# The recurrence's output copy behind the state's transposition and scaling, and the memory attention's Newton steps on VectorE

## The chip, the cores and the metric

The kernel runs on one core of one Trainium2 chip. The metric is the device time of one execution in microseconds (us), the median over several executions. The engines that matter are TensorE (PE, its weight loads shown apart as PEld), VectorE (DVE), ScalarE (ACT), GpSimd (POOL) and SyncE (SP, which issues the DMAs).

## The reference, cut to what matters

Two blocks follow each other, with 512 tokens of width 1024. The first mixes attention over the tokens and a context with a convolution. The second, with which this change has most to do, runs a delta-rule recurrence over 12 heads of width 64, beside it an attention of the tokens over 256 memory tokens, then an output projection and a feed-forward network.

```
def step(S, inp):                        # the recurrence, one token
    r_t, w_t, k_t, v_t, a_t, b_t = inp
    sa = einsum('bhvk,bhk->bhv', S, a_t)
    S = (S * w_t[:, :, None, :] + sa[..., None] * b_t[:, :, None, :]
         + v_t[..., None] * k_t[:, :, None, :])
    return S, einsum('bhvk,bhk->bhv', S, r_t)

def memory_cross_attention(q_mem, k_mem, v_mem, q_g, k_g):
    q = rms_norm_2(q_mem.reshape(B, T, MEM_HEADS, MEM_HEAD_DIM), q_g)
    k = k_mem * k_g                      # k_mem is rms-normed too
    s = einsum('bthd,bmhd->bhtm', q, k) * MEM_HEAD_DIM ** -0.5
    return einsum('bhtm,bmhd->bthd', softmax(s), v_mem)
```

## The kernel before, in words

Float32 products are made as three fp32r products of a high and a low part (`mm3`, `proj`), so each weight block (`wr`, by DMA) is split by ACT into `wh` and by DVE into `wl`. All instructions are given to a scheduling layer, which follows the order of the source by priority but moves an instruction past others where it reckons that an engine would wait; it also adds the semaphores. Within one PSUM bank it puts the accesses of any two engines one behind the other, in the order of the source. An engine works through its own list strictly in order, so an instruction that waits holds up all that stand behind it. Any edit to one engine's work can shift places in the lists of all.

The program has three stages in the trace: the first block (0 to 331 us), the second block's recurrence with the memory attention (331 to 767 us), and the feed-forward network (to 1120 us).

**The recurrence** runs over six pairs of heads, eight chunks of 64 tokens each. `gen_abc` makes each chunk's matrices (tiles `f`, `UX`, `E`, `W`, `QG`), and `gen_chain` carries the state from chunk to chunk. Its step works in one PSUM tile `yp` (tag `y`, a single buffer): four products of `E` and `UV` and one of the state `st` with `QG` give 64 columns of output and 64 of new state. Then DVE masks the state columns into `sb`, ACT copies the output columns into `y` (a tile `x` in the trace), PE transposes `sb` back into columns 128 to 255 of the same `yp`, and DVE scales that into the next `st`. The next step's products need the single `yp` free. There are 48 steps, 42 with a transposition. A table of due times (`CHAIN`, `TAIL` and others) sets the order in which the source emits these pieces among projections and the tail.

**The memory attention** (`memory`, in the tail) projects the memory tokens (`pj<-p`), takes `rm`, the memory rows' factor, then `rq` for the queries (16 columns) and `rk` for the keys (8 columns), both through `newton`, an inverse square root by three Newton steps, in 15 instructions on 128 x n tiles (tag `nr`). The first is always on DVE, the other 14 are on the engine that it is given: two to set up and four for each step. Both calls give it GpSimd. DVE then scales the keys by `rk` (`kn`, tag `p`, eight instructions and two copies). Three other calls of `newton` matter: the first block's attention (44 columns, on DVE), the first pair's `prep` (8 columns, on DVE), and the other pairs' `prep` and `finish` on GpSimd.

Of the kernel before, what the change touches and what calls it, by code (L numbers as in the profile page):

```python
# [16 lines left out]
AF = mybir.ActivationFunctionType  # L17
ALU = mybir.AluOpType
# [112 lines left out]
def flat(x):  # L131
    n = len(x.shape)
    if n == 2:
        return x
    if n == 3:
        return x.rearrange("p a b -> p (a b)")
    return x.rearrange("p a b c -> p (a b c)")
# [61 lines left out]
class SumSq:  # L199
# [12 lines left out]
    def rstd(self, ptag, inv, eps, r, eng=None):  # L212
        k = self.k
        n = self.w // P
        ss = k.t(ptag)
        for t in range(n):
            k.T.matmul(ss[:, t:t + 1], self.prev[:, t * P:(t + 1) * P], inv, start=True, stop=True)
        if eng is None:
            rsqrt(k, r, ss[:, :n], eps)
        else:  # L220
            newton(k, eng, r, ss[:, :n], eps)
        return r
# [7 lines left out]
def newton(k, G, r, x, eps=None, floor=None):  # L230
    n = x.shape[-1]
    xe, h, y, t = (k.t("nr", [n]) for _ in range(4))
    k.V.tensor_scalar(out=xe, in0=x, scalar1=floor if eps is None else eps, scalar2=None, op0=ALU.max if eps is None else ALU.add)
    G.tensor_scalar(out=h, in0=xe, scalar1=-0.5, scalar2=None, op0=ALU.mult)
    G.tensor_scalar(out=y.bitcast(I32), in0=xe.bitcast(I32), scalar1=-0.5, scalar2=float(0x5f3759df), op0=ALU.mult, op1=ALU.add)
    for i in range(3):
        G.tensor_tensor(out=t, in0=y, in1=y, op=ALU.mult)
        G.tensor_tensor(out=t, in0=t, in1=h, op=ALU.mult)
        G.tensor_scalar(out=t, in0=t, scalar1=1.5, scalar2=None, op0=ALU.add)
        G.tensor_tensor(out=r if i == 2 else y, in0=y, in1=t, op=ALU.mult)  # L240


class Norm:
# [96 lines left out]
def block1(k, I, st, h1d):  # L340
# [291 lines left out]
    for i in range(4):  # L632
# [4 lines left out]
        zgates(1)  # L637
    nrq = k.cal([32])
    newton(k, V, r44, ss44, 1e-6)
    V.tensor_scalar(out=rq, in0=rq, scalar1=0.125, scalar2=None, op0=ALU.mult)  # L640
    V.tensor_scalar(out=nrq, in0=rq, scalar1=-1.0, scalar2=None, op0=ALU.mult)
# [224 lines left out]
def prep(k, p, pd, wa, lw):  # L866
# [6 lines left out]
    for t in range(4):  # L873
        T.matmul(kss[:, 2 * t:2 * t + 2], sq[:, t * P:(t + 1) * P], k.sel2, start=True, stop=True)
    rn = k.t("s8", [8])
    newton(k, k.G if p else k.V, rn, kss[:, 0:8], floor=1e-24)
    yield
    ps = k.t("pj")
# [209 lines left out]
def gen_chain(k, p, pd, gi):  # L1088
    A, V, T = k.A, k.V, k.T
    mm = T.matmul  # L1090
    if gi == 0:
        pd["y"] = k.x()
    y = pd["y"]
    for cc in range(4 * gi, 4 * gi + 4):
        n, c = (cc // 2) % 2, cc % 2
        E, UV4, QG = pd[("g", gi)]
        yp = k.t("y")
        for h in range(2):
            u = 2 * h + n
            mm(yp[h * 64:h * 64 + 64, 0:P], UV4[:, u, c, :], flat(E[:, 2 * u + c]), start=True, stop=cc == 0)  # L1100
        if cc > 0:
            mm(yp[:, 0:P], pd["st"], QG[:, n, c, :], start=False, stop=True)
        if cc < 7:
            sb = k.t("sb", [2, 64])
            V.tensor_tensor(out=sb, in0=yp[:, 64:128].rearrange("p (o d) -> p o d", o=1).to_broadcast([P, 2, 64]),
                            in1=k.maskS.rearrange("p (c d) -> p c d", c=2), op=ALU.mult)
        A.activation(y[:, cc * 64:(cc + 1) * 64], yp[:, 0:64], AF.Copy)
        if cc < 7:
            T.transpose(yp[:, 128:256], flat(sb), k.ident)
            pd["st"] = k.t("st", [P])  # L1110
            V.tensor_scalar(out=pd["st"], in0=yp[:, 128:256], scalar1=pd["pc"][:, cc:cc + 1], scalar2=None, op0=ALU.mult)
        yield


# [27 lines left out]
def memory(k, I, qd, ssq, W):  # L1142
    A, V, T, Y = k.A, k.V, k.T, k.Y
# [22 lines left out]
    rm = ss.rstd("i", k.inv1k, 1e-6, k.cal([2]))  # L1166
    ssk = k.cal([8])
    rk, rq, nrq = k.cal([8]), k.cal([16]), k.cal([16])
    newton(k, k.G, rq, ssq, 1e-6)
    V.tensor_scalar(out=rq, in0=rq, scalar1=0.125, scalar2=None, op0=ALU.mult)  # L1170
    V.tensor_scalar(out=nrq, in0=rq, scalar1=-1.0, scalar2=None, op0=ALU.mult)
    kvs = []
    for t in range(2):
# [3 lines left out]
        sq = k.t("z", [4, 64])  # L1177
        A.activation(flat(sq), kv[:, :256], AF.Square, scale=0.125)
        V.tensor_reduce(out=ssk[:, 4 * t:4 * t + 4], in_=sq, op=ALU.add, axis=AX.X)
    newton(k, k.G, rk, ssk, 1e-6)  # L1180
    yield
    kns = []
    for t in range(2):
        kn = k.t("p", [4, 2, 64])
        for h in range(4):
            V.scalar_tensor_tensor(out=kn[:, h, 0, :], in0=kvs[t][:, h * 64:(h + 1) * 64], scalar=rk[:, 4 * t + h:4 * t + h + 1],
                                   in1=k.gg, op0=ALU.mult, op1=ALU.mult)
# [88 lines left out]
def block2(k, I, nm, h1d, out):  # L1276
# [47 lines left out]
    def tail():  # L1324
# [29 lines left out]
        Y.dma_start(out=gw, in_=I["g2"])  # L1354
        yield
        mem = memory(k, I, qd, ssq, W)
        for _ in range(10):
            next(mem)
# [26 lines left out]
    for p in range(6):  # L1385
        b = 2 * L * p
        at(prep(k, p, pds[p], wa, lw), *[b + r for r in PREP])
        at(project(p), *[b + LEAD[p] + PJ[0] + PJ[1] * i for i in range(3 * PIECES)])
        for gi in range(2):
            r0 = b + gi * L  # L1390
            at(gen_abc(k, p, pds[p], gi), *[r0 + i for i in range(16)])
            at(gen_chain(k, p, pds[p], gi), *[r0 + r for r in CHAIN])
        at(finish(k, p, pds[p]), *[b + L + r for r in FINISH])
# [215 lines left out]
```

## Time and profile before

| | |
|---|---|
| Time, median of 3 runs | 1121.05 us (1117.35 to 1123.47) |
| The profiled execution | 1122.11 us, span 1120.3 us |
| Mean granted TensorE clock | 0.986 |
| PE / DVE / ACT / POOL busy | 1077.6 / 727.6 / 538.0 / 61.8 us |

The span goes from the first to the last instruction of the profiled execution; 1.8 us of its time lie outside it. PE is busy nearly all the time, so what is to be read is when it is not, and when its clock is not full.

### The profile page before, as it was taken

What the parts mean: (1) busy time and instruction counts of PE and PEld (TensorE: products, weight loads), DVE (VectorE), ACT (ScalarE), POOL (GpSimd) and SP (SyncE); (2) the same over time, 40 slices, a digit from 0 to 9 for tenths busy, and PEclk for the clock granted to TensorE, in tenths of its full rate; (3) what the DMA queues carried; (4) which work ended last, traced back from release to release, by engine and by line L of the source; (5) the groups of instructions that cost most, each with busy time, mean ns of one, the idle gap of its engine ahead of it and who ended that gap; (6) DMA issues with size and microseconds to landing.
All of it is one profiled execution on the core that took longest, in us unless ns stands there. A gap on an engine that the chain in (4) does not pass through costs nothing.

```text
span 1120.3 us, 15945 instructions
## 1 busy us (share of the span) xinstructions
PE 1077.6 (96%) x6272; PEld 831.9 (74%) x6272; DVE 727.6 (65%) x1267; ACT 538.0 (48%) x987; POOL 61.8 (6%) x209
## 2 busy tenths in 40 slices
PE   8999989999999999999999879999999999999998
PEld 4668966666787677777777657768888888888887
DVE  3369999995776889797867877666444344344332
ACT  5444546765655556555455655555333133134110
POOL 0000000000010201122101121010000000000000
PEclk9999999999999999999999998999999999999999
DMA  9753221001362110110011212122323333333332
GB/s 330 286 178 105 64 81 45 1 23 35 94 199 90 57 39 20 39 37 28 32 39 52 67 48 76 40 74 85 104 94 94 94 96 101 103 95 94 94 122 85
DMA packets 32203, 96.46 MB, mean 86 GB/s; under 512 B 3456, under 2 KB 6272, under 8 KB 32128
## 3 DMA queue, kind: packets, MB, share of 16 engines
q1 hardware_dynamic: 32128, 95.45, 26.5%
q8 instruction: 49, 0.80, 0.3%
q14 instruction: 26, 0.21, 0.1%
HBM read 91.24 MB, written 4.19 MB: 85 GB/s over the span
## 4 chain that ended last, share of the span: by engine, by line
PE 82%; DVE 6%; ACT 4%; POOL 3%; DMA 3%; issue 2%; SPq 0%; ACTq 0%; DVEq 0%; POOLq 0%
PE pf L57 31%; PE pj L57 22%; PE s L57 9%; PE i L57 7%; PE pt L57 5%; PE pv L57 4%; PE y L57 3%; POOL nr L57 3%; DMA modw<-w_mod 1%; ACT p L57 1%; DVE wl L57 1%; DVE hg L57 1%; ACT wh L57 1%; DVE p L57 1%; DMA wr<-w_in 1%
## 5 line engine op out<-in xcount | busy, mean ns | idle before, releaser
L57 ACT ACTIVATE wh<-wr 128x1024 fp32r<-128x1024 f32 (+1 forms) x132 | 137.7, 1043 | 183.7 <-PE pf L57 73.9
L57 DVE TENSOR_TENSOR wl<-wr,wh 128x1024 fp32r<-128x1024 f32 (+1 forms) x132 | 158.7, 1203 | 21.9 <-PE pt L57 10.2
L57 PE MATMUL pf<-A,wh 128*128 128x512 f32 x512 | 157.8, 389 | 0.0
L57 PE MATMUL pj<-hg,wh 128*128 128x512 f32 x448 | 152.5, 412 | 1.4 <-DVE x L57 0.9
L57 ACT ACTIVATE f<-i 128x512 f16<-128x512 f32 (+1 forms) x132 | 71.9, 598 | 90.1 <-PE i L57 89.9
L57 PEld LDWEIGHTS pf<-A,wh 128*128 128x128 f32 x512 | 96.0, 188 | 19.7
L57 PE MATMUL pf<-A,wl 128*128 128x512 f32 x256 | 99.6, 389 | 0.0
L57 DVE TENSOR_TENSOR x<-x,pf 128x512 f32<-128x512 f32 (+1 forms) x33 | 22.2, 671 | 113.9 <-PE pf L57 113.9
L57 PEld LDWEIGHTS pj<-hg,wh 128*128 128x128 f32 x448 | 80.2, 190 | 18.5 <-issue 2.2
L57 PE MATMUL pj<-hg,wl 128*128 128x512 f32 x224 | 90.2, 403 | 0.0
L57 DVE SCALAR_TENSOR_TENSOR hg<-hg,c 128x499 f32<-128x499 f32 (+14 forms) x120 | 84.9, 738 | 0.7 <-ACT hg L57 0.4
L57 PE MATMUL pf<-ff,wh 128*128 128x512 f32 (+1 forms) x272 | 79.6, 377 | 0.0
L57 PE MATMUL pf<-hg,wh 128*128 128x512 f32 x256 | 78.8, 389 | 0.0
L57 DVE SCALAR_TENSOR_TENSOR fr<-pf,r 128x512 f32<-128x512 f32 x32 | 22.1, 691 | 85.4 <-PE pf L57 82.1
L57 ACT ACTIVATE fr<-fr 128x512 f32<-128x512 f32 x32 | 20.2, 632 | 99.9 <-DVE fr L57 99.9
L57 PEld LDWEIGHTS <-f 128*128 128x128 f16 x720 | 46.8, 101 | 24.1 <-issue 13.7
L57 PE MATMUL i<-f 128*128 128x128 f16 x672 | 56.2, 226 | 5.3 <-DVE f L57 4.9
L57 PEld LDWEIGHTS pf<-ff,wh 128*128 128x128 f32 x272 | 50.1, 188 | 9.4
L57 PEld LDWEIGHTS pf<-A,wl 128*128 128x128 f32 x256 | 48.0, 188 | 10.1
L57 PEld LDWEIGHTS pf<-hg,wh 128*128 128x128 f32 x256 | 48.0, 188 | 9.9
L57 PE MATMUL pf<-ff,wl 128*128 128x512 f32 (+1 forms) x136 | 51.2, 376 | 0.0
L57 PE MATMUL pf<-hg,wl 128*128 128x512 f32 x128 | 49.8, 389 | 0.0
(312 smaller groups left out, 2114.8 us busy)
## 6 DMA issues: line engine op xcount, KB each, us to landing
wr<-w_ff SPq DMA_DIRECT2D x64, 512.0 KB, 3.5
modw<-w_mod SPq DMA_DIRECT2D x20, 512.0 KB, 7.6
wr<-rw_in SPq DMA_DIRECT2D x20, 512.0 KB, 3.6
wr<-w_in SPq DMA_DIRECT2D x10, 512.0 KB, 3.7
wr<-w_out SPq DMA_DIRECT2D x8, 512.0 KB, 3.6
wr<-w_start SPq DMA_DIRECT2D x8, 384.0 KB, 5.9
x<-xT SPq DMA_DIRECT2D x8, 256.0 KB, 5.8
modw<-w_mod SPq DMA_DIRECT2D x8, 256.0 KB, 6.2
```

The costliest lines, as they stand in the source:

```text
L57: r = f(*a, **kw)
```

## The change

In `newton`, when the engine is VectorE, each step's addition of 1.5 and the multiplication behind it become one instruction. `memory` gives both of its calls VectorE. In `gen_chain`, the output copy is emitted behind the transposition and the scaling of the state.

```
@@ newton @@
     for i in range(3):
         G.tensor_tensor(out=t, in0=y, in1=y, op=ALU.mult)
         G.tensor_tensor(out=t, in0=t, in1=h, op=ALU.mult)
-        G.tensor_scalar(out=t, in0=t, scalar1=1.5, scalar2=None, op0=ALU.add)
-        G.tensor_tensor(out=r if i == 2 else y, in0=y, in1=t, op=ALU.mult)
+        if G is k.V:
+            G.scalar_tensor_tensor(out=r if i == 2 else y, in0=t, scalar=1.5, in1=y, op0=ALU.add, op1=ALU.mult)
+        else:
+            G.tensor_scalar(out=t, in0=t, scalar1=1.5, scalar2=None, op0=ALU.add)
+            G.tensor_tensor(out=r if i == 2 else y, in0=y, in1=t, op=ALU.mult)
@@ gen_chain @@
-        A.activation(y[:, cc * 64:(cc + 1) * 64], yp[:, 0:64], AF.Copy)
         if cc < 7:
             T.transpose(yp[:, 128:256], flat(sb), k.ident)
             pd["st"] = k.t("st", [P])
             V.tensor_scalar(out=pd["st"], in0=yp[:, 128:256], scalar1=pd["pc"][:, cc:cc + 1], scalar2=None, op0=ALU.mult)
+        A.activation(y[:, cc * 64:(cc + 1) * 64], yp[:, 0:64], AF.Copy)
         yield
@@ memory @@
-    newton(k, k.G, rq, ssq, 1e-6)
+    newton(k, V, rq, ssq, 1e-6)
@@
-    newton(k, k.G, rk, ssk, 1e-6)
+    newton(k, V, rk, ssk, 1e-6)
```

Where it moves instructions: first VectorE in the memory attention, from the start of the queries' Newton steps on. Before, `c2_2987` in the fifth row is `rq`, made by GpSimd and scaled here by two instructions, and the state's mask `sb` stands behind it.

```order
L57 TENSOR_SCALAR nr_7149<-c2_2987 128x16
L57 TENSOR_TENSOR wl_7601<-wr_7599,wh_7600 128x1024
L57 TENSOR_TENSOR QG_7121<-AR_5694,s_7112 128x4x64
L57 TENSOR_TENSOR QG_7121<-g_58,s_7112 128x4x64
L57 TENSOR_SCALAR c2_2987<-c2_2987 128x16 x2
L57 TENSOR_TENSOR sb_7203<-y_7199,g_58 128x128
L57 TENSOR_TENSOR f_7214<-i_7209,c2_2987 128x512
```

Now, in the same place on VectorE:

```order
L57 TENSOR_TENSOR QG_7115<-g_58,s_7106 128x4x64
L57 TENSOR_SCALAR nr_7144<-nr_7143 128x16
L57 TENSOR_SCALAR nr_7145<-nr_7143 128x16
L57 TENSOR_TENSOR nr_7146<-nr_7145 128x16
L57 TENSOR_TENSOR nr_7146<-nr_7146,nr_7144 128x16
L57 TENSOR_TENSOR sb_7191<-y_7187,g_58 128x128
L57 SCALAR_TENSOR_TENSOR nr_7145<-nr_7146,nr_7145 128x16
L57 TENSOR_TENSOR f_7202<-i_7197,c2_2984 128x512
L57 TENSOR_TENSOR nr_7146<-nr_7145 128x16
L57 TENSOR_SCALAR st_7194<-y_7187,s8_5608 128x128
```

The mask `sb` and the scaled state `st` now stand among the Newton steps and ahead of the finished `rq`, no longer behind it.

Second, VectorE at the keys' Newton steps. Before, the scaling of the keys by `rk` (`p<-p,c2`) stands ahead of `f_7287`, a tile of the next pair's inverse.

```order
L57 TENSOR_TENSOR f_7268<-f_7264,c2_2987 128x512
L57 SCALAR_TENSOR_TENSOR p_7270<-p_7170,c2_2987 128x64 x4
L57 SCALAR_TENSOR_TENSOR p_7276<-p_7175,c2_2987 128x64
L57 COPY p_7270<-p_7270 128x4x64
L57 SCALAR_TENSOR_TENSOR p_7276<-p_7175,c2_2987 128x64 x3
L57 TENSOR_TENSOR f_7287<-i_7282,c2_2987 128x512
```

Now, in the same place, where `f_7275` is that tile:

```order
L57 TENSOR_TENSOR f_7256<-f_7252,c2_2984 128x512
L57 TENSOR_TENSOR nr_7174<-nr_7174,nr_7172 128x8
L57 TENSOR_TENSOR f_7275<-i_7270,c2_2984 128x512
L57 SCALAR_TENSOR_TENSOR nr_7173<-nr_7174,nr_7173 128x8
L57 TENSOR_TENSOR x_3807<-x_3807,pj_7294 128x512
L57 TENSOR_TENSOR nr_7174<-nr_7173 128x8
```

The inverse's tile has moved ahead of the keys' scaling, which follows some nine rows later.

Third, TensorE at a step of the chain shortly before the memory attention (`y<-g,sb` is the transposition, `y<-E,UV` the next step's first products). Before:

```order
L57 MATMUL y_6603<-g_58,sb_6607 128x128
L57 LDWEIGHTS f_6585
L57 MATMUL i_6643<-f_6624,f_6585 128x128
L57 LDWEIGHTS f_6585
L57 MATMUL i_6643<-f_6624,f_6585 128x128
L57 LDWEIGHTS f_6585
L57 MATMUL i_6643<-f_6624,f_6585 128x128
L57 LDWEIGHTS f_6585
L57 MATMUL i_6643<-f_6624,f_6585 128x128
L57 MATMUL y_6657<-E_5597,UV_5679 64x128 x2
```

Now:

```order
L57 LDWEIGHTS f_6588
L57 MATMUL i_6630<-f_6595,f_6588 128x128
L57 MATMUL y_6597<-g_58,sb_6601 128x128
L57 MATMUL y_6651<-E_5591,UV_5673 64x128 x2
L57 MATMUL y_6651<-QG_6353,st_6604 128x128
```

The four products that stood between the transposition and the next step's first products now stand behind them.

## Rows read from the trace of the kernel before

**Rows 1.** The page's part 1: busy time, share of the span, instructions of each engine

```profile
PE 1077.6 (96%) x6272; PEld 831.9 (74%) x6272; DVE 727.6 (65%) x1267; ACT 538.0 (48%) x987; POOL 61.8 (6%) x209
```

**Rows 2.** Windows of 28 us: PE, PEld, DVE, ACT, POOL busy, granted clock, DMA

```profile
616.00:644.00 28.00, 24.63 (x208) 18.20 (x206) 22.50 (x47) 17.45 (x45) 2.94 (x14) 0.94 0.21 67
644.00:672.00 28.00, 22.41 (x161) 16.29 (x158) 21.44 (x55) 15.79 (x34) 7.47 (x28) 0.93 0.15 48
672.00:700.00 28.00, 27.03 (x205) 19.86 (x206) 20.39 (x43) 13.84 (x35) 2.94 (x14) 0.83 0.25 76
```

**Rows 3.** Windows of 2 us in the memory attention, same columns

```profile
658.00:660.00 2.00, 0.34 (x5) 0.14 (x2) 0.52 (x4) 0.00 (x0) 1.09 (x5) 1.00 0.00 0
...
662.00:664.00 2.00, 2.00 (x12) 1.28 (x11) 1.37 (x4) 1.74 (x4) 0.00 (x0) 0.50 0.00 0
...
670.00:672.00 2.00, 0.00 (x0) 0.00 (x0) 2.00 (x10) 0.04 (x1) 0.00 (x0) 0.88 0.00 0
...
674.00:676.00 2.00, 2.00 (x15) 1.68 (x13) 1.53 (x4) 1.19 (x4) 0.00 (x0) 0.50 0.00 0
```

**Rows 4.** Waits: engine line <- releaser: us in total, times, longest

```profile
ACT x L57 <- DVE sb L57: 9.6, 5, 3.0
...
PE y L57 <- ACT x L57: 4.8, 4, 2.4
```

**Rows 5.** Timeline, 616 to 621 us: start, us, engine, instruction [idle before <-releaser]

```profile
617.11 0.29 DVE L57 TENSOR_TENSOR sb<-y,g 128x128 f32<-128x128 f32 x1
...
617.46 1.06 ACT L57 ACTIVATE wh<-wr 128x1024 fp32r<-128x1024 f32 x1
...
619.05 0.22 ACT L57 ACTIVATE x<-y 128x64 f32<-128x64 f32 x1
...
619.33 0.33 PE L57 MATMUL y<-g,sb 128*128 128x128 f32 x1 [2.36 <-ACT x L57]
...
619.70 0.35 DVE L57 TENSOR_SCALAR st<-y,s 128x128 f32<-128x128 f32 x1 [0.21 <-PE y L57]
...
620.11 0.52 PE L57 MATMUL y<-E,UV 128*64 128x128 f32 x4 [0.22 <-DVE st L57]
```

**Rows 6.** Timeline, 654 to 661 us, at the queries' Newton steps

```profile
654.25 1.44 POOL L57 TENSOR_SCALAR nr<-nr 128x16 f32<-128x16 f32 x2 [21.97 <-DVE nr L57]
...
656.70 0.44 PE L57 MATMUL y<-QG,st 128*128 128x128 f32 x2
...
659.20 0.22 POOL L57 TENSOR_TENSOR c<-nr 128x16 f32<-128x16 f32 x1
659.45 0.39 DVE L57 TENSOR_SCALAR c<-c 128x16 f32<-128x16 f32 x2 [3.49 <-POOL c L57]
659.74 0.28 DVE L57 TENSOR_TENSOR sb<-y,g 128x128 f32<-128x128 f32 x1
...
660.34 0.33 PE L57 MATMUL y<-g,sb 128*128 128x128 f32 x1 [2.00 <-ACT x L57]
```

**Rows 7.** Timeline, 665 to 673 us, at the keys' Newton steps

```profile
665.76 0.28 DVE L57 TENSOR_TENSOR sb<-y,g 128x128 f32<-128x128 f32 x1
...
669.77 1.07 DVE L57 SCALAR_TENSOR_TENSOR p<-p,c 128x64 f32<-128x64 f32 x5 [0.97 <-POOL c L57]
...
671.55 0.68 DVE L57 TENSOR_TENSOR f<-i,c 128x512 f16<-128x512 f32 x1
...
672.29 2.85 PE L57 MATMUL i<-f 128*128 128x128 f16 x24 [3.15 <-DVE f L57]
```

**Rows 8.** Timeline of DVE, 356 to 359 us: the first pair's Newton steps

```profile
356.22 0.17 DVE L57 TENSOR_SCALAR nr<-nr 128x8 f32<-128x8 f32 x1
356.43 0.57 DVE L57 TENSOR_TENSOR nr<-nr 128x8 f32<-128x8 f32 x3
```

**Rows 9.** Timeline, 155 to 157 us: the first block's attention

```profile
155.17 0.73 PE L57 MATMUL pj<-U,wh 128*128 128x512 f32 x2 [2.60 <-DVE hg L57]
...
156.01 3.63 ACT L57 ACTIVATE kn<-kn,c 128x128 f32<-128x128 f32 x12 [2.04 <-DVE c L57]
```

## The prediction

> **What bounds the kernel now.** I read the page's part 1 first: the reader is to see that PE is busy for 96% of the span [rows 1], so that a change helps only where PE stands idle or runs at its lower clock. The windows of 28 us say where that is. Behind the recurrence PE is without a gap; the poorest stretch of the whole program is 644 to 672 us, with 22.41 us busy of 28 [rows 2], and that is the memory attention. The same rows give the granted clock: 0.94, 0.93 and 0.83 in three neighbouring stretches. The windows of 2 us show what these means are made of: PE does nearly nothing at 658 to 660 and nothing at 670 to 672, and soon after each it works at 0.50, that is at 1.2 instead of 2.4 GHz [rows 3]. So an idle stretch costs twice, once as idle time and once as slow work after it. In the three stretches of [rows 2] the lower clock takes 28 x (0.06 + 0.07 + 0.17) = 8.4 us, nearly all of it after three idle stretches: 2.36 us at 617, 2.00 us at 658 and 3.15 us at 669 [rows 5 to 7].
>
> Next I followed each of the three back through its timeline. At 658, GpSimd works on the queries' Newton steps from 654.25 to 659.42. DVE's scaling of `rq` waits 3.49 us for the last of them, and the chain's mask `sb` stands behind it in DVE's list, although its own input, PE's product with `QG`, was done at 657.14. So `sb` starts at 659.74, the output copy and PE's transposition after it, at 660.34 [rows 6]. At 669, DVE waits 0.97 us for GpSimd's `rk`, then does the keys' scaling, and only at 671.55 the tile `f` for which PE has been waiting [rows 7]. At 617 no GpSimd is involved: the mask is done at 617.40, but ACT has a weight block and another tile ahead of the output copy, which comes at 619.05, and the transposition waits for it [rows 5].
>
> **The first edit, the output copy.** In the old order the copy waits for the mask (9.6 us in five long waits of ACT) and the transposition for the copy (4.8 us of PE in four) [rows 4]. It reads other columns than either of its neighbours, so the waits come from the single PSUM tile that all of them share. The copy still has to be done before the next step's products overwrite that tile, and the tile has one buffer. So the step keeps its five links, products, mask, transposition, scaling, copy; the copy is only moved from the third place to the last. Its cost per step was 0.22 us and about a tenth for the hand-over before the transposition, and is the same before the next products.
>
> A rule that bears on this: the Trainium skill, PSUM — Partial Sum Buffer, section "PSUM bank collisions raise a hardware error", says that two engines must be kept apart by bank and not by address. By that rule the copy cannot leave the chain, and the edit's sum is 0; read by columns, it would leave it, and the edit would save what PE waits for it. The waits of [rows 4] agree with the rule.
>
> What it does at 617 can be followed. The transposition can start at about 617.45. The next products, which now stand right behind it, need the copy, and ACT's list ahead of that is as long as before, to 619.05. They start near 619.35 instead of 620.11 [rows 5], with the four small products that stood before them already done or still to do behind them. I take 0.7 us. The clock's loss after it (0.06 x 28 = 1.7 us) I leave in place, since most of the idle time stays.
>
> At the other 41 steps the bound on one side is all that PE waits for the copy, 4.8 - 2.36 - 2.00 = 0.4 us to gain beyond the two long ones. On the other side, where the next products follow the transposition at once, PE now waits for scaling and copy, 0.35 + 0.22 and two hand-overs, against scaling alone before: 0.3 us more. If half of 41 steps are so bare, that is 6 us. In most steps of the order other products lie between them, and the scheduler has moved some of them there, so I take 0 and keep -0.4 to +6 as bounds.
>
> **The second edit, Newton on VectorE.** It takes 14 instructions from GpSimd and puts 11 on DVE, twice. A dependent one costs DVE 0.2 us from start to start [rows 8], so 2.2 us each if alone, against 659.42 - 654.25 = 5.2 us on GpSimd [rows 6]; 4.4 us of DVE work are added in all. In the stretch from 644 to 672 DVE is busy 21.44 of 28 us [rows 2], part of its idle time being the very waits that go, so I count this work at nothing; without that cover it would cost up to 4.4 us.
>
> The queries: `sb` no longer stands behind `rq`, but behind four of the Newton steps, which end before its input is there at 657.14. It ends near 657.5, the transposition starts at 657.55. Behind `sb` on DVE stand a Newton step (0.2), an `f` tile (0.68, as in [rows 7]), another step (0.1 of which shows) and the scaling (0.35 [rows 5]): `st` near 658.8, the copy near 659.1, and only then the next products. PE has six small products between the two, of 0.1 us at most (24 such took 2.85 us at the lower clock [rows 7]), so it idles from about 658.1 to 659.1: 1.0 us instead of 2.00, a gain of 1.0 us. Half of an idle stretch that was followed by the low clock is left. I take it that the clock then stays up, which gives 28 x 0.07 = 2.0 us, of which I count 1.7 here (the rest, in the last two us of the stretch, belongs to the next one).
>
> The keys: from `sb` to the tile `f` it was 671.55 - 665.76 = 5.8 us. Of that, 0.97 was the wait for GpSimd and 1.78 the keys' scaling (669.77 to 671.55) [rows 7]; both are now behind `f`. Seven Newton instructions have come in between, and put between other work such an instruction delays it by about 0.12 us each (0.2 less what overlaps): 0.8 us. So 5.8 - 0.97 - 1.78 + 0.8 = 3.8 us, 2.0 us sooner, and PE's 3.15 us of idle time become about 1.1. The keys' scaling is late next: it comes after eight further rows of DVE, but PE takes the keys' transpositions only far behind, so that hides it; if it did not, the price is those rows and its own time, 4 x 0.68 + 4 x 0.12 + 1.78 = 5 us. The clock's loss here is 28 x 0.17 = 4.8 us and spans three times the other one; with some idle time left I count half, 2.4, bounds 0 and 4.8.
>
> **What else moves.** The fused step also shortens the first block's Newton (three instructions of 0.2 us, 0.6 us of DVE) and the first pair's. There ACT waits 2.04 us for the result, but PE waits 2.60 us for another DVE instruction, a gate that frees its bank [rows 9], and that gate stands behind a weight split as before. I take 0.6 us, bounds 0 and 2.0. And the lists of all engines are rearranged from there on, in the first block's attention most of all. A stall like that of [rows 9], with a stretch of low clock like the 1.7 us above behind it, is worth 4 us; one more or one less of them is what I allow for this, with 0 as the value.
>
> **The sum.** 0.7 + 1.0 + 1.7 + 2.0 + 2.4 + 0.6 = 8.4 us. The profiled execution took 1122.1 us, of which 1.8 lie outside the span, and is 1.1 us above the median of 1121.05. From 1122.1 this gives 1113.7; by the median it would be 1112.6. I say **1113 us**. A measurement of this kernel tells about 0.5% from no change, 5.6 us: 1115.4 and 1126.7 are the borders.
>
> **The rivals.**
> The idle time goes, the clock does not come back. What is left of each idle stretch (1.0 and 1.1 us) is followed by the low clock as before; for it speaks that 0.50 stands after a row of 2 us that was 0.34 busy and not wholly idle [rows 3]. Then 0.7 + 1.0 + 2.0 + 0.6 = 4.3 us are left, 1117.8 us: no change that can be told.
> The first edit does what its words say and takes the copy out of the chain. For it speaks that all 4.8 us of PE's waits [rows 4] name the copy; against it the single buffer. It would take the 2.36 us at 617 whole with its 1.7 us of clock, in place of my 0.7, and 0.4 elsewhere: 3.8 us more, about 1110.
> The copy, now last, holds back the next products at nearly every step. At 0.3 us for each of 41 bare steps it costs 12 us, and where such waits bring the clock down once or twice more, 3 us besides: 1113.7 + 15, about 1128, slower. It decides from some 28 bare steps on, where the second edit's gain is used up. For it speaks the order at 617, where the next products have come right behind the transposition; against it that most steps have other products there.
>
> **How the numbers follow.** The forecast has a chance of 0.52 (its own range 1107 to 1117), the clock that stays low 0.29, the copy out of the chain 0.10, the copy that holds back every step 0.09. The first and the third end mostly below 1115.4, the second within 0.5%, the last beyond 1126.7 for the most part. That makes 0.57 faster, 0.35 the same, 0.08 slower. The range reaches up over the second case and leaves out the last: 1105 to 1121.
>
> **What would show it.** In the changed kernel's trace DVE should wait for no GpSimd at the memory attention, the two idle stretches of PE there should be about 1 us each, and the granted clock of the stretch behind the second should rise from 0.83. At 617 the transposition should no longer wait for the copy, and the next products should. Waits of PE's `y` products for `x` of over 8 us in total would show the fourth case. A new stall of PE in the first block's attention, between 150 and 270 us, would make the prediction wrong without touching its steps.

## The result and the profile after

The changed kernel took 1114.74 us (median of 16, 1110.57 to 1124.38) against 1120.18 us for the kernel before (16 runs beside it): the medians differ by 5.4 us. The ratio estimated from all of these runs, by which kernels are compared below, is 0.9941, with a 95% interval of 0.9924 to 0.9958, which is 6.6 us less. The profiled execution took 1114.73 us, its span 1112.9 us.

The page's part 1 of the changed kernel, to be held against [rows 1]: GpSimd has 28 instructions less, DVE 16 more. (`L57` in the rows below is the line of a helper through which every instruction passes; the tile names tell them apart.)

```profile
PE 1074.0 (97%) x6272; PEld 835.0 (75%) x6272; DVE 727.8 (65%) x1283; ACT 539.5 (48%) x987; POOL 55.4 (5%) x181
```

The windows of 28 us of the changed kernel, same columns as [rows 2], to be held against the last two there:

```profile
644.00:672.00 28.00, 23.67 (x177) 16.57 (x176) 24.29 (x78) 14.53 (x35) 0.00 (x0) 0.80 0.10 31
672.00:700.00 28.00, 28.00 (x216) 21.75 (x219) 20.31 (x40) 17.50 (x39) 2.96 (x14) 0.96 0.26 81
```

PE is busier in the memory attention (23.67 us against 22.41) and GpSimd has gone from it, but the clock is lower there (0.80 against 0.93). The program has moved forward by some 8 us here, so a window no longer holds the same work as before: the lower clock that [rows 2] have behind 672 us (0.83) now lies ahead of it. Windows that hold the same work stand in the part on the prediction.

The waits of the changed kernel in the second block, where [rows 4] stand for before:

```profile
ACT x L57 <- DVE st L57: 15.5, 20, 2.9
...
PE y L57 <- ACT x L57: 3.7, 4, 1.5
```

The copy, now last, waits for the scaling (20 waits of ACT). PE still waits for the copy four times, but now it is the next products that wait.

The place that [rows 5] show, in the timeline of the changed kernel:

```profile
611.17 0.28 DVE L57 TENSOR_TENSOR sb<-y,g 128x128 f32<-128x128 f32 x1
...
611.51 0.33 PE L57 MATMUL y<-g,sb 128*128 128x128 f32 x1 [0.48 <-DVE sb L57]
...
613.34 0.69 PE L57 MATMUL y<-E,UV 128*64 128x128 f32 x4 [1.51 <-ACT x L57]
```

The transposition comes 0.34 us behind the mask's start, not 2.2 us as before, and the products wait for ACT instead: 1.99 us of idle time where there were 2.36 and 0.22.

The memory attention in the timeline of the changed kernel, for [rows 6, 7]; PE first, then DVE:

```profile
657.98 0.33 PE L57 MATMUL y<-g,sb 128*128 128x128 f32 x1 [0.49 <-DVE sb L57]
659.33 0.44 PE L57 MATMUL y<-E,UV 128*64 128x128 f32 x4 [1.01 <-ACT x L57]
...
661.25 1.94 PE L57 MATMUL i<-f 128*128 128x128 f16 x16 [0.47 <-DVE f L57]
663.61 1.01 PE L57 MATMUL i<-f 128*128 128x128 f16 x8 [0.42 <-ACT f L57]
...
666.50 0.48 PE L57 MATMUL y<-g,sb 128*128 128x128 f32 x1 [0.60 <-DVE sb L57]
667.68 0.69 PE L57 MATMUL y<-E,UV 128*64 128x128 f32 x4 [0.70 <-ACT x L57]
...
657.65 0.28 DVE L57 TENSOR_TENSOR sb<-y,g 128x128 f32<-128x128 f32 x1
...
660.51 0.68 DVE L57 TENSOR_TENSOR f<-i,c 128x512 f16<-128x512 f32 x1
...
664.39 1.06 DVE L57 SCALAR_TENSOR_TENSOR p<-p,c 128x64 f32<-128x64 f32 x5
...
666.16 0.29 DVE L57 TENSOR_TENSOR sb<-y,g 128x128 f32<-128x128 f32 x1
```

No single stretch of 2 or 3 us is left; there are six pieces of 0.4 to 1.0 us. From the mask to the tile `f` it is 2.86 us instead of 5.79. What is late now is the next mask: the keys' scaling (`p<-p,c`) stands ahead of it on DVE. One window over this piece of the changed kernel shows how full DVE is here:

```profile
652.00:668.00 16.00, 12.29 (x99) 8.72 (x95) 15.64 (x57) 9.14 (x23) 0.00 (x0) 0.77 0.06 17
```

DVE is busy for 15.64 us of 16. For the kernel before, the window from 654 to 672 us, which holds both waits for GpSimd, has 12.08 of 18 on DVE and 7.47 on GpSimd.

### The profile page after: what moved, and what is told of

Its sections match the earlier page's. It is cut to its first block, busy times and chain, and to the rows that moved or that the text cites. A ratio compares the mean times of both kernels' runs of the same rounds, so it can differ in the third digit from the quotient of the medians.

```text
span 1112.9 us, 15943 instructions
## 1 busy us (share of the span) xinstructions
PE 1074.0 (97%) x6272; PEld 835.0 (75%) x6272; DVE 727.8 (65%) x1283; ACT 539.5 (48%) x987; POOL 55.4 (5%) x181
## 4 chain that ended last, share of the span: by engine, by line
PE 84%; DVE 8%; ACT 5%; issue 1%; DMA 1%; POOL 0%; SPq 0%; ACTq 0%; DVEq 0%; POOLq 0%
PE pf L57 31%; PE pj L57 23%; PE s L57 9%; PE i L57 8%; PE pt L57 5%; PE pv L57 4%; PE y L57 3%; DVE wl L57 1%; DVE hg L57 1%; DVE p L57 1%; ACT tA L57 1%; ACT p L57 1%; DVE f L57 1%; ACT xb L57 1%; DVE c L57 1%
## 5 line engine op out<-in xcount | busy, mean ns | idle before, releaser
L57 ACT ACTIVATE wh<-wr 128x1024 fp32r<-128x1024 f32 (+1 forms) x132 | 137.5, 1042 | 182.8 <-PE pf L57 67.0
L57 DVE TENSOR_TENSOR wl<-wr,wh 128x1024 fp32r<-128x1024 f32 (+1 forms) x132 | 158.8, 1203 | 22.2 <-PE pt L57 10.0
L57 PE MATMUL pf<-A,wh 128*128 128x512 f32 x512 | 157.8, 389 | 0.0
L57 PE MATMUL pj<-hg,wh 128*128 128x512 f32 x448 | 155.8, 417 | 1.4 <-DVE x L57 0.9
L57 PEld LDWEIGHTS pf<-A,wh 128*128 128x128 f32 x512 | 96.0, 188 | 19.7
L57 ACT ACTIVATE f<-i 128x512 f16<-128x512 f32 (+1 forms) x132 | 71.3, 597 | 80.0 <-PE i L57 80.0
L57 PE MATMUL pf<-A,wl 128*128 128x512 f32 x256 | 99.6, 389 | 0.0
L57 DVE TENSOR_TENSOR x<-x,pf 128x512 f32<-128x512 f32 (+1 forms) x33 | 22.2, 672 | 113.9 <-PE pf L57 113.9
L57 PEld LDWEIGHTS pj<-hg,wh 128*128 128x128 f32 x448 | 81.0, 190 | 19.2 <-issue 3.0
L57 PE MATMUL pj<-hg,wl 128*128 128x512 f32 x224 | 90.5, 404 | 0.0
L57 DVE SCALAR_TENSOR_TENSOR hg<-hg,c 128x504 f32<-128x504 f32 (+14 forms) x120 | 84.9, 739 | 0.7 <-ACT hg L57 0.4
L57 PE MATMUL pf<-ff,wh 128*128 128x512 f32 (+1 forms) x272 | 79.7, 377 | 0.0
L57 PE MATMUL pf<-hg,wh 128*128 128x512 f32 x256 | 78.7, 389 | 0.0
L57 DVE SCALAR_TENSOR_TENSOR fr<-pf,r 128x512 f32<-128x512 f32 x32 | 22.1, 692 | 85.4 <-PE pf L57 82.1
L57 ACT ACTIVATE fr<-fr 128x512 f32<-128x512 f32 x32 | 20.2, 632 | 99.8 <-DVE fr L57 99.8
L57 PEld LDWEIGHTS <-f 128*128 128x128 f16 x720 | 47.5, 102 | 23.4 <-issue 14.7
L57 PE MATMUL i<-f 128*128 128x128 f16 x672 | 56.4, 226 | 3.5 <-DVE f L57 3.0
L57 PEld LDWEIGHTS pf<-ff,wh 128*128 128x128 f32 x272 | 50.1, 188 | 9.4
L57 PEld LDWEIGHTS pf<-A,wl 128*128 128x128 f32 x256 | 48.1, 188 | 10.0
L57 PEld LDWEIGHTS pf<-hg,wh 128*128 128x128 f32 x256 | 48.1, 188 | 9.9
L57 PE MATMUL pf<-ff,wl 128*128 128x512 f32 (+1 forms) x136 | 51.2, 376 | 0.0
L57 PE MATMUL pf<-hg,wl 128*128 128x512 f32 x128 | 49.8, 389 | 0.0
```

What stands on the lines that cost most here:

```text
L57: r = f(*a, **kw)
```

## The experiments

Each ratio is against runs of the kernel before on the same chip, with its 95% interval. The two edits and the fused step within the second make three parts that can each be there or not, and all eight combinations were timed:

| fused step | Newton on VectorE | copy in its old place | copy moved |
|---|---|---|---|
| no | no | 1 (before) | 0.9990 |
| yes | no | 0.9967 | 0.9984 |
| no | yes | 1.0005 | 0.9921, and 0.9928 again |
| yes | yes | 0.9999 | 0.9941 (the change) |

**The copy alone (chain_only).**

```
 before.py with the copy's activation behind the scaling; newton() as before
```

> First edit alone: the output copy behind the scaling in the recurrence's step; the Newton steps as before. Theory A (my terms): the edit is worth 0.7 us at the place at 617 and nothing at the other steps, so 1119.5 against 1120.2. Theory B (the copy was a link of every step, and the recurrence before the memory attention, which came out some 6 us shorter in the changed kernel, owes that to this edit): 1113 to 1115. Theory C (lists merely rearranged, with low-clock stretches of PE falling elsewhere): anywhere between 1116 and 1124, and the part of the span that differs need not be the recurrence.

Measured: 0.9990 (0.9976 to 1.0003), 1119.63 us. The total fits theory A, but for another reason than A gave. A pair of heads in the recurrence has a steady period, from one group of eight small `pj<-g,p` products to the next but one (each pair has two such groups). Windows cut there, for the kernel before and then for this one, show it:

```profile
452.85:504.87 52.02, 50.22 (x422) 37.37 (x422) 43.59 (x87) 29.42 (x68) 9.02 (x28) 1.00 0.11 31
504.87:557.15 52.28, 50.21 (x421) 37.36 (x421) 43.58 (x87) 29.43 (x68) 9.02 (x28) 1.00 0.10 32
```

```profile
454.17:504.72 50.55, 49.58 (x421) 37.48 (x421) 43.47 (x87) 29.50 (x68) 9.45 (x28) 1.00 0.11 33
504.72:555.28 50.56, 49.59 (x421) 37.48 (x421) 43.49 (x87) 29.50 (x68) 9.45 (x28) 1.00 0.10 32
```

The clock is at its full 2.4 GHz in all four. Two pairs took 104.30 us before and take 101.11 us now: theory B's gain, 1.5 to 1.7 us a pair. The grouped lines of the same two periods (before, then this kernel) say where it comes from:

```profile
L57 PE MATMUL i<-R,UX 128*128 128x128 f32 x16 | 2.3, 281 | 0.6 <-DVE UX L57 0.6
L57 PE MATMUL y<-g,sb 128*128 128x128 f32 x7 | 2.2, 317 | 0.2 <-ACT x L57 0.2
```

```profile
L57 PE MATMUL i<-R,UX 128*128 128x128 f32 x16 | 2.3, 278 | 0.0
L57 PE MATMUL y<-g,sb 128*128 128x128 f32 x7 | 2.0, 281 | 0.0
```

The idle time that names the copy is only 0.2 us of it. A wait for another DVE tile (0.6 us) goes too, and the rest lies in time that counts as PE's busy time (50.22 against 49.58). The step itself shows why the copy mattered, though PE hardly waits for it by name. Timelines of one step of the second period, before (DVE, two rows of ACT, PE) and in this kernel (DVE, PE):

```profile
520.68 0.28 DVE L57 TENSOR_TENSOR sb<-y,g 128x128 f32<-128x128 f32 x1
...
521.22 1.57 ACT L57 ACTIVATE f<-i 128x512 f16<-128x512 f32 x3 [1.27 <-PE i L57]
522.67 0.24 ACT L57 ACTIVATE x<-y 128x64 f32<-128x64 f32 x1
...
522.97 0.33 PE L57 MATMUL y<-g,sb 128*128 128x128 f32 x1
```

```profile
520.37 0.29 DVE L57 TENSOR_TENSOR sb<-y,g 128x128 f32<-128x128 f32 x1
...
521.15 0.27 PE L57 MATMUL y<-g,sb 128*128 128x128 f32 x1
```

Before, the copy stands in ACT's list behind three tiles that wait for PE, and the transposition starts 2.29 us after the mask; now it starts 0.78 us after it. Over the seven transpositions of this period the distance from mask to transposition falls from 11.2 to 7.1 us. PE has other products for most of that time, so 1.5 to 1.7 us of it reach the period.

Part of the gain is then lost in the memory attention. In its timeline, PE's row of the transposition, PE's row of the tile `f` and DVE's second wait for GpSimd:

```profile
653.77 0.33 PE L57 MATMUL y<-g,sb 128*128 128x128 f32 x1 [1.95 <-DVE sb L57]
...
667.02 2.85 PE L57 MATMUL i<-f 128*128 128x128 f16 x24 [4.05 <-DVE f L57]
...
664.50 1.07 DVE L57 SCALAR_TENSOR_TENSOR p<-p,c 128x64 f32<-128x64 f32 x5 [1.87 <-POOL c L57]
```

The work ahead of the keys' Newton steps comes sooner, so DVE waits 1.87 us for GpSimd instead of 0.97, and PE 4.05 us instead of 3.15 [rows 7]. From the transposition on, PE's waits there come to 8.0 us, where the kernel before has 6.3. Another 1.8 us go in the last stretch of the recurrence, between the last two pairs' second groups of small products: 50.94 us (679.07 to 730.01) against 49.16 (683.99 to 733.15), at a granted clock of 1.00 in both.

**The Newton steps alone (newton_only) and without the fused step (mem_only).**

```
 before.py with
-    newton(k, k.G, rq, ssq, 1e-6)
+    newton(k, V, rq, ssq, 1e-6)      # rk likewise; newton_only: newton() fused too
```

> Second edit alone: the memory attention's Newton steps on VectorE with the fused third step, the copy in its old place. Theory A (my terms): 1.0 + 2.0 from shorter idle stretches of PE, 0.6 from the first block, and up to 4.1 from the clock: 1112.5 to 1116.6 against 1120.2. Theory B (the recurrence's gain is the first edit's): only the memory attention's 3 to 4 us less what the stretch behind it gives back, 1117 to 1120.

> The memory attention's Newton steps on VectorE, four instructions to a step, alone: the copy in its old place, nothing fused. Theory E (the two edits hang together: moved alone, the copy's gain of some 1.6 us a pair is eaten where DVE waits for GpSimd, and the Newton steps alone leave the recurrence's pairs at 52 us): pairs of 52.0 to 52.3 us, no wait of DVE for GpSimd, 0.997 to 1.000 of before. Theory F (the gain of 0.992 with both edits unfused is the Newton steps' own): 0.993 to 0.995.

Measured: 0.9999 (0.9978 to 1.0021) and 1.0005 (0.9982 to 1.0028). This is theory E (and B's range for newton_only); theory A, which gave this edit nearly the whole gain, falls for it alone. In mem_only the pairs keep their old period:

```profile
453.04:505.06 52.02, 50.20 (x422) 37.38 (x422) 43.59 (x87) 29.45 (x68) 9.04 (x28) 1.00 0.10 32
```

DVE waits for no GpSimd there, and PE's long idle stretches are gone. But the mask's transposition waits for the copy again, and short waits stand in their place. The first of them, in the timeline of PE in mem_only:

```profile
664.84 0.33 PE L57 MATMUL y<-g,sb 128*128 128x128 f32 x1 [0.85 <-ACT x L57]
```

They come to 4.4 us, where the kernel before has 6.3, so in this execution 1.9 us of idle time are gained here. As much is lost in the last stretch of the recurrence: 51.23 us (679.73 to 730.96) against 49.16 before, at a granted clock of 1.00 in both.

**The fused step alone (fused_only), and the change without the memory part (chain_fused).**

```
 fused_only: before.py with the fused branch in newton(); chain_fused: and the copy moved
```

> Only the fusing of the Newton steps that are on VectorE anyway, in the first block and in the recurrence's first pair; the copy and the memory attention as before. Theory A (my term): 0.6 us, 1119.6. Theory C: in the changed kernel the first block was up to 4.8 us ahead at 270 us and had lost all of it by 300 us; if that comes from this edit alone, this kernel shows the same two shifts and stays at 1120 within 1 us at 330 us, and what its lists do behind that decides the rest.

> The changed kernel with the memory attention's Newton steps back on GpSimd (copy moved, first block's Newton fused). Theory A (my terms): it lacks 1.0 + 2.0 us of idle time and the clock's part, so it is 3 to 7 us behind the changed kernel: 0.997 to 1.000 of before. Theory B (sizes as the single edits gave them, 0.999 x 0.9967): 0.996. Theory D (the memory edit gains nothing at all once PE's total idle time and its low clock are counted, as fused_only against newton_only suggests): as the changed kernel, 0.994, or below it.

Measured: 0.9967 (0.9950 to 0.9984) and 0.9984 (0.9964 to 1.0004). The first is more than either theory gave. Half of its 3.7 us has a place in the trace: the stretch up to the first pair's end, whose first Newton steps are on DVE, takes 99.63 us (351.31 to 450.94) and took 101.49 before (351.36 to 452.85). It is shorter in the other three pairs of kernels that differ in the fusing alone too, 99.62 against 101.44, 98.76 against 101.40 and 100.18 against 101.37. That is more than the 0.6 us of my term, and in another place than the first block, from whose three instructions the term was worked out. Whether the three instructions less or the other order of the lists give it was not traced. Over the four pairs of kernels that differ in the fusing alone its effect is -0.33, -0.06, -0.06 and +0.17% (the last against the mean of the two runs), in the mean -0.8 us. Each of these differences is uncertain by some 0.3%, and the clock has a part in them (see mem_unfused). The second run bears theory A out: the changed kernel is 0.43% ahead of chain_fused, 4.8 us, and theory D (that the memory part gains nothing) falls.

**One Newton chain at a time (rq_only, rk_only).**

```
 the change with one of the two back on GpSimd:
 rq_only: newton(k, V, rq, ...), newton(k, k.G, rk, ...); rk_only the other way round
```

> The changed kernel with only the queries' Newton steps on VectorE, the keys' on GpSimd. Theory A: the idle stretch before the tile f stays near 3 us and the low clock behind it stays, so 2.0 to 4.4 us behind the changed kernel, 0.996 to 0.998 of before. Theory D: as the changed kernel, 0.994.

> The changed kernel with only the keys' Newton steps on VectorE, the queries' on GpSimd. Theory A: the mask stands again behind the queries' scaling, an idle stretch of 2 us of PE comes back ahead of the transposition; 1.0 to 2.7 us behind the changed kernel, 0.995 to 0.9965 of before. Theory D: as the changed kernel, 0.994.

Measured: 0.9954 (0.9933 to 0.9974) and 0.9958 (0.9939 to 0.9976), 1.5 and 1.9 us behind the change, within or near theory A's ranges. Against chain_fused (0.9984) each alone gives some 3 us and both together 4.8: they share part of a gain. PE's rows in rq_only (first) and rk_only show the stretch that stays in each:

```profile
662.27 2.85 PE L57 MATMUL i<-f 128*128 128x128 f16 x24 [5.20 <-DVE f L57]
```

```profile
654.68 0.48 PE L57 MATMUL y<-g,sb 128*128 128x128 f32 x1 [1.93 <-DVE sb L57]
```

With the queries' wait gone and the keys' left, the second idle stretch grows to 5.20 us: much of what one wait gave is waited for at the next.

**The change without the fused step (mem_unfused), twice.**

```
-        if G is k.V:
-            G.scalar_tensor_tensor(out=r if i == 2 else y, in0=t, scalar=1.5, in1=y, ...)
-        else:
         G.tensor_scalar(...)
         G.tensor_tensor(...)
```

> The changed kernel with four instructions to a Newton step in place of three on VectorE (no fusing anywhere). Theory A (my term 0.6 and six more instructions of 0.16 us in the memory attention, half of them in the open): 1 us behind the changed kernel, 0.995. Theory B (the fusing alone gave 3.7 us, by the lists that it rearranges): 3 to 4 us behind it, 0.997 to 0.998.

> The changed kernel without the fusing once more, beside finish_v on the same chip: 0.992 of before if the first measurement holds; 0.994 if it differs from the changed kernel by nothing but its share of low-clock stretches in those executions.

Measured: 0.9921 (0.9896 to 0.9946) and 0.9928 (0.9902 to 0.9954), 1112.22 and 1113.16 us, on two chips. Both theories expected it behind the change; it is at least level with it, and with the best ratio of all kernels (its interval and that of the change overlap). DVE has six instructions more in the memory attention, and their order is another one. In its timeline, DVE:

```profile
662.31 0.29 DVE L57 TENSOR_TENSOR sb<-y,g 128x128 f32<-128x128 f32 x1
...
663.29 0.86 DVE L57 SCALAR_TENSOR_TENSOR p<-p,c 128x64 f32<-128x64 f32 x4
```

The keys' Newton steps end later, so the mask now goes ahead of their scaling, and PE's transposition there waits for nothing, where the change has 0.60 us. Yet PE's idle time in the memory attention is not less: its waits come to 4.4 and 4.9 us in the two profiles and to 3.7 us in the change. What is better is the clock. The granted clock over the span is 0.994 in both profiles, against 0.983 for the change and 0.986 before; over all executions its mean is 0.991 and 0.990, against 0.985 in the 16 of the change. Executions at the same mean clock come nearer to the work alone, though the mean does not say on which work the low clock fell: at 0.991 this kernel took 1113.0 to 1113.6 us (three executions), the change 1110.7 and 1111.5, and the kernel before 1118.3 to 1119.3 (five). So at the same clock it is some 2 us behind the change, between the two theories, and its higher clock makes up for that. Why its clock is higher was not found.

**The copy made twice (copy_twice).**

```
+        A.activation(y[:, cc * 64:(cc + 1) * 64], yp[:, 0:64], AF.Copy)
         A.activation(y[:, cc * 64:(cc + 1) * 64], yp[:, 0:64], AF.Copy)
```

> The changed kernel with the output copy made twice in each of the recurrence's 48 steps (the second writes the same values again). Theory A (in the changed kernel the copy, now last, lies beside other products of PE except at the few places where PE waits for it): a pair of heads keeps its period of 50.55 us, PE's four waits for x grow by 0.2 us each, and the time by 1 us, 0.995 of before. Rival (the copy ends each step in the open): 0.22 us at each of 42 steps, a period of 52 us and some 9 us in all, 1.002 of before.

Measured: 0.9985 (0.9964 to 1.0007), 0.44% or 4.9 us behind the change, between the two. The period answers the question that it was for:

```profile
502.82:553.70 50.88, 49.96 (x421) 37.73 (x421) 43.46 (x87) 31.04 (x76) 9.46 (x28) 1.00 0.11 32
```

Eight more copies, 1.5 us more work on ACT, lengthen a pair by 0.33 us, not by 1.8 (the pair ahead of it took 52.50 us at a granted clock of 0.97): in the steady recurrence the copy, now last, lies beside other products. PE's four waits for it grow from 3.7 to 4.8 us, as theory A had it. The other 3 to 4 us of this kernel were not traced to one place; its mean clock over 12 executions, 0.985, is that of the change.

**The transposition in a bank of its own (own_bank).**

```
-            T.transpose(yp[:, 128:256], flat(sb), k.ident)
+            tp = k.t("i")
+            T.transpose(tp[:, 0:P], flat(sb), k.ident)
```

> The changed kernel with the state's transposition in a PSUM tile of its own (another bank) in place of columns 128 to 255 of the step's tile, so that copy, transposition and scaling no longer share a bank. Theory A (engines are kept apart within a bank, so the copy remained a link of the step): ACT's waits of 15.5 us for the scaling vanish, the next products wait for the copy less than 3.7 us, the step loses its copy of 0.22 us and one hand-over, and the time falls by 0 to 4 us, 1111 to 1115 against 1114.7. Theory B (the copy is hidden behind other products at nearly every step): within 1 us of 1114.7. Against both, tiles of that tag are taken from the recurrence's matrices, which could cost 2 to 6 us.

Measured: 1.0022 (1.0004 to 1.0040), slower than the change by 0.8%, more than expected against it. The copy is no longer behind the scaling; its waits name the mask instead. But the transposition now takes one of the three `i` tiles that the matrices also use, PE waits longer for the mask there, and the period of a pair rises to 51.70 and 52.50 us. Waits of this kernel, second block:

```profile
ACT x L57 <- DVE sb L57: 23.8, 14, 3.9
...
PE i L57 <- DVE sb L57: 7.7, 6, 2.1
```

So it shows that taking the tile there costs more than it gives. That the shortage of `i` tiles is the cause is argued, not shown, and what a free bank would give stays open.

**The last pair's Newton steps too (finish_v).**

```
 mem_unfused with
-    newton(k, k.G, gr, gss[:, 0:8], 64e-5)
+    newton(k, V if p == 5 else k.G, gr, gss[:, 0:8], 64e-5)
```

> The changed kernel without the fusing (as mem_unfused), with the last pair's Newton steps of its final normalisation on VectorE too, where PE stands idle 0.86 us before the last output projection. Theory A: GpSimd's 14 instructions take 2.9 us there and 12 on DVE about 2, so PE's idle time of 0.86 us goes and 0.9 us are gained, 0.991 of before. Rival (something else, the earlier stall of 1.28 us for ACT, ends last there): nothing, 0.992.

Measured: 0.9931 (0.9908 to 0.9953), beside 0.9928 for mem_unfused on the same chip: nothing, the rival. PE's two rows there are unchanged, 1.28 us and 0.86 us, in finish_v:

```profile
725.94 1.05 PE L57 MATMUL pj<-g,p 128*128 128x2 f32 x8 [1.28 <-ACT p L57]
738.20 0.73 PE L57 MATMUL pj<-hg,wh 128*128 128x512 f32 x2 [0.86 <-DVE x L57]
```

## Why the prediction was right, and where its steps were not

The time came out 1.7 us above the 1113 that was said, and on the forecast's side. The forecast gain was 8 us from 1121.05; beside the change the kernel before had a median of 1120.18, so 5.4 us were gained by the medians and 6.6 by the ratio. The sum was about right; its parts were not: 4.1 of its 8.4 us were for a clock that did not come back, and a gain that it had put at nothing stands in their place. That the two nearly cancel is luck.

**The place at 617** behaved as worked out: 2.36 + 0.22 us of idle time became 0.48 + 1.51, 0.6 us for a term of 0.7.

**"I take 0" for the other 41 steps is the step that failed.** The bound on the gain, 0.4 us, was PE's idle time that names the copy. The runs show 1.5 to 1.7 us for each steady pair, 3.2 us over the two that can be measured cleanly, and in every kernel with one copy, moved, and the bank kept: 50.55 against 52.02 us (50.54 in mem_unfused, 50.55 in the change's first such pair; its second took 52.13 us at a granted clock of 0.97). The forecast counted 0.22 us and a tenth for the copy in each step. What the transposition really stood behind was the copy's place in ACT's list: in the seven steps of a period the copy starts 0.32 to 2.09 us after the mask does. What this delayed showed as a wait for another tile and inside PE's busy time, and only 0.2 us of it as a wait for the copy. Behind the scaling it costs almost nothing (copy_twice). The rule that I weighed, the Trainium skill, PSUM — Partial Sum Buffer, section "PSUM bank collisions raise a hardware error", keeps engines apart by bank. The trace still agrees with it: the copy waits for the scaling, in other columns of the same bank, 20 times for 15.5 us, and in own_bank it does not. These waits are set by the scheduling layer, which goes by bank too; what the chip would do without them no run here shows. What I drew from it, a sum of 0, was wrong: a link that cannot leave the chain can still be moved to where the chain has slack.

**The queries' wait**: the term was 1.0 us. The step that had 2.00 us now has none, and the one behind it has 0.49 + 1.01 where it had 0.45: 0.95 us. That wait and two later ones, in the timeline of PE before:

```profile
667.58 0.44 PE L57 MATMUL y<-E,UV 128*64 128x128 f32 x4 [0.45 <-DVE st L57]
...
678.55 2.07 PE L57 MATMUL pj<-x,g 128*128 128x512 f32 x2 [0.31 <-ACT x L57]
681.84 1.16 PE L57 MATMUL i<-R,UX 128*128 128x128 f32 x8 [0.36 <-DVE UX L57]
```

**The keys' wait**: the term was 2.0 us. `f` comes 2.86 us behind the mask, better than the 3.8 worked out. But that the keys' scaling comes late is not hidden by the distance to the keys' transpositions, as the forecast had it: it delays the next mask, and PE idles 0.60 + 0.70 us there. The 3.15 us and the two later waits, 3.8 in all, became 0.47 + 0.42 + 0.60 + 0.70 = 2.2, a gain of 1.6 us.

**The clock**, 1.7 + 2.4 us, did not come back in the profiled execution. PE worked at 0.50 right behind the pieces that were left. Windows of 2 us of the changed kernel, for [rows 3]:

```profile
658.00:660.00 2.00, 0.99 (x7) 0.61 (x7) 2.00 (x9) 0.22 (x1) 0.00 (x0) 1.00 0.00 0
660.00:662.00 2.00, 1.53 (x18) 1.20 (x17) 2.00 (x9) 1.13 (x3) 0.00 (x0) 0.66 0.00 0
...
672.00:674.00 2.00, 2.00 (x11) 2.00 (x11) 0.91 (x2) 1.30 (x3) 0.00 (x0) 0.50 0.00 0
```

So the rival "the clock does not come back" was right about the clock, in this execution and in the mean: 0.985 over the 16 executions of the change, 0.986 to 0.987 over the 87 of the kernel before that stood beside the other runs. The time still came out near the forecast with the recurrence's gain in the clock's place. In both profiles of mem_unfused the clock did come back (0.994 over the span). One profile each cannot tell how much of the difference between kernels is clock, but executions at the same clock can: at 0.991 the change is some 8 us ahead of the kernel before (the times stand at mem_unfused), more than the 6.6 us measured over all.

**DVE's added work**, counted at nothing, fills DVE to 15.64 of 16 us. That did not stop the gain; the pieces of idle time that are left wait for DVE's rows or for ACT's behind them, which fits a full list on DVE as their cause. **Three new waits** took something back, which no step foresaw: 0.48 us of the next products for the copy at 636 us, 0.62 us ahead of the memory attention, and 1.28 us before the last pair's small products (0.18 before). Timeline of PE, changed kernel:

```profile
647.84 0.73 PE L57 MATMUL pj<-wh,p 128*128 128x512 f32 x2 [0.62 <-DVE p L57]
...
725.70 1.05 PE L57 MATMUL pj<-g,p 128*128 128x2 f32 x8 [1.28 <-ACT p L57]
```

**The reshuffle** was put at 0 with 4 us either way. The new wait of 1.28 us and the fusing's total effect of -0.33 to +0.17% stay within that. **The fused step**, 0.6 us, gave nothing in the first block: the first pair's first small products behind it start at 351.36 us before and at 351.45 now. From there to the first pair's end the four pairs of kernels show 1.2 to 2.6 us.

Windows that hold the same work (PE's instruction counts agree) give the whole difference of 7.4 us between the two profiled spans its place. Columns as in [rows 2], before and then the changed kernel:

```profile
557.15:683.99 126.84, 115.10 (x880) 88.15 (x880) 93.12 (x196) 70.09 (x161) 18.86 (x70) 0.91 0.16 48
683.99:733.15 49.16, 48.97 (x333) 35.79 (x331) 32.79 (x62) 27.03 (x67) 2.94 (x14) 1.00 0.25 80
```

```profile
554.31:675.03 120.72, 111.82 (x880) 86.34 (x880) 95.04 (x218) 70.90 (x163) 11.44 (x42) 0.92 0.16 50
675.03:725.70 50.67, 49.39 (x334) 36.11 (x332) 33.22 (x63) 27.65 (x67) 2.96 (x14) 1.00 0.25 78
```

Up to 351 us the two are level, and again in all that follows these rows (387.15 and 387.20 us). The stretch from there to the first pair's end gains 1.3 us and the two steady pairs 1.6, since the lower clock fell into the second of them. The stretch with the place at 617 and the memory attention gains 6.1 us, and the last one loses 1.5. Of the 6.1 us, 2.8 are idle time of PE, of which the pieces named above make 0.6 + 0.95 + 1.6 - 0.48 - 0.62 = 2.05. The other 3.3 lie in PE's busy time, with the same number of instructions at a mean clock of 0.92 instead of 0.91; how much of that is clock and how much is delay inside PE's busy time stays open.

What no term contained is how the two edits hang together. With the Newton steps on GpSimd, moving the copy gives -0.10 and +0.17%; with them on VectorE, -0.58 and -0.81%. Moving the Newton steps gives 0.05 and 0.32% more time with the copy in its old place, and 0.43 and 0.66% less with it moved. That makes some 8 us which neither edit has alone. Two parts of it are seen. In chain_only, part of what the recurrence saves is waited for at GpSimd. And the last stretch of the recurrence takes 49.16 us before and in fused_only, but 50.67 to 51.31 us in the other six kernels of the table, at a granted clock of 1.00 in all: either edit alone pays these 1.5 to 2.2 us, and both together pay them only once. All six show the wait of 1.28 us for ACT there, 1.1 us more than before; why either edit brings it on was not traced. That these two parts and the clock are the whole cause is argued, not shown.

The copy as a link at nearly every step (the fourth case) is out: PE's waits for `x` are 3.7 us, below the 8 that it needed. The copy out of the chain (the third) is out as well: the copy waits for the scaling 20 times.

## What to carry to other kernels

Price a link in a repeated step by the period of the steady loop, cut at the same instruction in both traces, and not by the idle time that names the link. Two waits in a row on a chain hide each other's worth: test edits together as well as alone, since two that are worth nothing apart gave 6 to 8 us here. When helper work moves onto an engine that the chain needs, look at which long instruction then comes ahead of the chain's next link. And where executions of one kernel differ in granted clock, compare kernels at the same clock before the order of their lists is called the cause.

## What the runs showed of the hardware that was not expected

A delay in PE's chain need not show as idle time: 0.64 us of the 1.47 us by which a pair got shorter lay in PE's busy time, with the same 421 or 422 instructions at the same granted clock. And pieces of 0.4 to 1.0 us of idle time, with PE 0.50 to 0.77 busy in rows of 2 us, were followed by the lower clock just as the stretches of 2 and 3 us that they replaced. Not always: in the second profile of mem_unfused PE was no busier in the same place, and the granted clock stayed at 1.00, as one of its windows of 4 us shows:

```profile
656.00:660.00 4.00, 1.86 (x17) 1.17 (x18) 4.00 (x20) 0.96 (x3) 0.00 (x0) 1.00 0.00 0
```

What decides between the two was not found.
